# Where the tiles that TensorE reads begin in a partition: one residue modulo 512 bytes in place of several, in a two-layer decoder trunk

## The chip, the cores and the metric

The kernel runs on one core of a Trainium2 chip. The metric is the device time of one execution in microseconds (us). Before the change it is 2214.95 us, the median of three runs (2213.07 to 2218.6).

The core's engines run side by side, each on its own queue of instructions: TensorE (PE for its matmuls, PEld for its weight loads), VectorE (DVE), ScalarE (ACT), GpSimd (POOL) and SyncE (SP), which here issues most of the DMAs. The on-chip memory has 128 partitions; a tile takes the same range of bytes in each of them. TensorE multiplies a stationary operand (the weights, 128 columns) with a moving one (up to 512 columns here) and adds into a bank of the accumulation memory.

## The reference

A trunk of two layers on a sequence of 1024 positions of width 1024, all in float32. The first layer mixes by a gated linear recurrence, the second by sliding-window attention; each is followed by a layer norm, a gated FFN with a short causal convolution, and a second layer norm.

```python
for layer in range(DEPTH):
    if layer < N_A_LAYERS:
        mix = hgrn2_mixer(h, hgrn_w_in[layer], lower_bounds[layer],
                          hgrn_gnorm_w[layer], hgrn_w_out[layer])
    else:
        j = layer - N_A_LAYERS
        mix = swa_sink_mixer(h, k_shared, v_shared, swa_w_q[j], swa_sinks[j],
                             bias, mask, swa_w_out[j])
    h = layer_norm(ALPHA * h + mix, ln_mix_g[layer], ln_mix_b[layer])
    ff = conv_ffn(h, ffn_w_in[layer], ffn_conv_w[layer], ffn_conv_b[layer], ffn_w_out[layer])
    h = layer_norm(ALPHA * h + ff, ln_ffn_g[layer], ln_ffn_b[layer])
    if layer == N_A_LAYERS - 1:
        k_flat, v_flat = jnp.split(h @ shared_w_kv, 2, axis=-1)
        ...
```

`conv_ffn` multiplies 1024 × 1024 by 1024 × 5632, runs a causal convolution of width 3 over each channel, gates one half with the SiLU of the other, and multiplies 1024 × 2816 by 2816 × 1024. The mixers project with 1024 × 1024 matrices (four of them in the recurrence, two in attention, and one shared for keys and values).

## The kernel before

**Split products.** Every large operand is kept as two parts, a rounded one (`hi`) and the rest (`lo`), written by ScalarE (a copy, L203 or L158) and VectorE (a subtraction, L151). `mm3` (L175 to L178) makes one product of three matmuls: hi by hi (L176), hi by lo (L177), lo by hi (L178). These three lines issue 9288 of the matmuls, 7560 of them with 512 moving columns and 1728 with 256. TensorE's order is that of the program, written out by hand.

**Tiles and their places.** Pools lay tiles one behind the other in a partition, in the order of allocation; a tile's size is rounded up to 32 bytes. The pool `cp` (L100 to L110) comes first and stays: after a pad it holds

- T, 65,536 bytes, the activations transposed, hi and lo; it begins at byte 2048 of a partition
- Y, 32,768 bytes, at byte 67,584
- HL, at byte 100,352: the buffer of split weights, 12 × 1024 + 256 floats. It has six places of 8192 bytes, HL0 to HL5, each with a hi and a lo row of 1024 floats. `STARTS` (L134) puts place i at 2048 i floats plus 0, 16, 32, 64, 128 or 256 floats, so that in bytes modulo 512 they begin at 0, 64, 128, 256, 0 and 0
- small tiles (`ident`, parameters, masks), and a last pad of 8 floats

The pool `sm` follows with 1024 bytes of small tiles. All later pools begin behind it, at byte 154,304, which is 192 modulo 512: the recurrence's tiles (`hp`); for each FFN the extra weight tile HT (three rows of 4096 bytes), the raw loads `rx0` to `rx2` and TX (49,152 bytes, combinations of activations) or R in its place; and for attention the raw loads and the pool `at`, whose K and QB stand at 192, X and Vt at 256, and W, `q` and `bf` at 320 modulo 512.

**Stages**, in order of time: the recurrence over eight heads (projections `qf` and `ig_block`, and short matmuls of `recur` between them); its output projection (`out_proj`, L321); the FFN's up-projection (`Up`), its down-projection (`Down`); then keys, values and attention; output projection; `Up`; `Down`.

- In projections of the recurrence and of attention, T is moving (512 columns) and a place of HL holds the weights (`proj_T`, `q_proj`), or T holds the weights and HL is moving with 256 columns (`proj_tok`). Places are taken in turn (`ring`).
- In `out_proj`, the first half of the columns has T as weights and HL0 to HL3 moving; the second half has T as weights and TX moving.
- In `Up`, 22 blocks of columns (fc) each make seven products of twelve matmuls (a 2 × 2 scheme with seven products in place of eight). The order of products is 1, 2, 6, 7, 4, 5, 3. `weight_load` gives an even fc the pieces 8 to 14 (HL4 for products 1 and 2, HT for 6 and 7, HL5 for 4 and 5, HT again for 3), and an odd fc the pieces 0 to 6 (HL0, HL2, HL1, HL3). Moving is T, then TX for 6 and 7, T, and TX for 3.
- In `Down`, seven products over eleven chunks and four blocks of rows, three matmuls each, have both operands in one place of 1024 + 1024 floats: one of fifteen, six in HL, one in HT and eight in T.

**The tile `nsk`** (L1146, L1147) holds the negated sinks for attention. It is made on GpSimd from `sk`, which a DMA on ScalarE's queue brings (L1114, L1115), behind the loads of the layer norm's rows and of the shared weights, and behind the splits of these weights. `attend` reads it at L1233. On GpSimd's queue the memsets of QB (L1111) stand ahead of it, and the powers of the layer norm (`rs`, L225) behind it.

## Time and profile before

| | us |
|---|---|
| median of three runs | 2214.95 |
| lowest and highest | 2213.07, 2218.6 |
| the profiled execution | 2223.18 |
| its span, first to last instruction | 2221.4 |
| TensorE matmul busy in the span | 2175.4 |
| VectorE busy | 1786.9 |
| ScalarE busy | 941.6 |

Of the profiled execution 1.8 us lie outside its span. A row of the profile's groups names line, engine, operation, output and inputs by the program's tile names, with moving operand ahead of weights for a matmul; then shapes and count, busy time and mean duration, and idle time before with what ended it. Matmuls overlap in the pipeline, so their durations add up to more than the time that they take; the distance from one start to the next is what one costs, and it is read from the order of time. HL stands there for all of its places: which one is read follows from the order in the program. L12 is line 12 of the kernel.

### The profile page before, as it was taken

How to read it: one execution, taken by the hardware profiler on the slowest of the kernel's cores; microseconds unless marked ns; L12 is line 12 of the kernel's file. 1: busy time of each engine (PE TensorE's matmuls, PEld its weight loads, DVE VectorE, ACT ScalarE, POOL GpSimd, SP SyncE). 2: the span in 40 equal slices, each digit the busy share in tenths (PEclk: the TensorE clock that was granted, in tenths of full speed). 3: DMA queues.
4: the chain of work that ended last, by engine and by line, in shares of the span. 5: the costliest groups of instructions: out<-in, count | busy, mean ns of one | idle time of the engine just before them, and what ended most of it. 6: DMA issues, size and time to landing. Idle time of an engine off the chain costs nothing.

```text
span 2221.4 us, 33413 instructions
## 1 busy us (share of the span) xinstructions
PE 2175.4 (98%) x13135; PEld 1815.6 (82%) x13135; DVE 1786.9 (80%) x2415; ACT 941.6 (42%) x1625; POOL 178.5 (8%) x200
## 2 busy tenths in 40 slices
PE   8999999999999999999999999999999999999998
PEld 7888888978888888887888888777788888888887
DVE  2777665565789888888998778887799888889987
ACT  3333323332744443343333456764654443343431
POOL 0121111110100000000000012211000000000001
PEclk9999999999999999999999999999999999999999
DMA  6555443252222222238854421114222222249663
GB/s 196 187 194 172 153 171 115 62 126 91 86 85 85 84 79 86 85 102 264 276 168 133 114 89 34 34 56 135 76 95 94 74 79 86 86 143 314 207 213 132
DMA packets 231945, 281.16 MB, mean 127 GB/s; under 512 B 29978, under 2 KB 160747, under 8 KB 228971
## 3 DMA queue, kind: packets, MB, share of 16 engines
q1 hardware_dynamic: 228736, 276.53, 38.2%
q10 hardware_dynamic: 3050, 2.49, 0.8%
q8 instruction: 103, 1.69, 0.3%
q14 instruction: 56, 0.45, 0.1%
HBM read 213.96 MB, written 65.01 MB: 126 GB/s over the span
## 4 chain that ended last, share of the span: by engine, by line
PE 73%; DVE 14%; ACT 5%; DMA 4%; issue 3%; POOL 1%; SPq 0%; ACTq 0%; DVEq 0%; POOLq 0%
PE psmm L176 15%; PE psmm L178 15%; PE psmm L177 15%; PE psax L176 8%; PE psax L178 8%; PE psax L177 8%; PE psax L182 3%; DVE T L151 2%; DVE HL L151 1%; DMA rx<-in_ffn_w_in_dram 1%; PE psax L186 1%; DVE Y L481 1%; ACT Y L251 1%; ACT T L203 1%; DVE QB L1198 1%
## 5 line engine op out<-in xcount | busy, mean ns | idle before, releaser
L176 PE MATMUL psmm<-T,HL 128*128 128x512 f32 x768 | 309.9, 404 | 0.0
L177 PE MATMUL psmm<-T,HL 128*128 128x512 f32 x768 | 301.6, 393 | 3.8 <-issue 2.0
L178 PE MATMUL psmm<-T,HL 128*128 128x512 f32 x768 | 301.9, 393 | 0.0
L481 DVE SCALAR_TENSOR_TENSOR Y<-Y,cwt 128x1023 f32<-128x1023 f32 (+1 forms) x176 | 225.1, 1279 | 40.0 <-ACT Y L479 39.8
L479 ACT ACTIVATE Y<-Y,cwt 128x1024 f32<-128x1024 f32 x88 | 108.8, 1237 | 262.1 <-DVE Y L468 258.2
L176 PE MATMUL psmm<-HL,T 128*128 128x256 f32 (+1 forms) x656 | 199.6, 304 | 2.3 <-ACT T L203 2.3
L178 PE MATMUL psmm<-HL,T 128*128 128x256 f32 (+1 forms) x656 | 195.0, 297 | 2.4 <-DVE T L151 2.4
L177 PE MATMUL psmm<-HL,T 128*128 128x256 f32 (+1 forms) x656 | 194.7, 297 | 1.2 <-DVE HL L151 1.2
L203 ACT CAST HL<-rx 128x1024 fp32r<-128x1024 f32 (+1 forms) x137 | 140.2, 1043 | 125.6 <-DMA rx<-in_ffn_w_in_dram 35.0
L151 DVE TENSOR_TENSOR HL<-rx,HL 128x1024 fp32r<-128x1024 f32 (+1 forms) x137 | 165.6, 1212 | 16.0 <-ACT HL L203 15.4
L178 PEld LDWEIGHTS psmm<-T,HL 128*128 128x128 f32 x768 | 144.8, 189 | 35.2 <-issue 2.2
L177 PEld LDWEIGHTS psmm<-T,HL 128*128 128x128 f32 x768 | 145.3, 189 | 31.6 <-DVE T L151 2.7
L176 PEld LDWEIGHTS psmm<-T,HL 128*128 128x128 f32 x768 | 144.9, 189 | 31.7 <-issue 1.5
L176 PE MATMUL psax<-T,HL 128*128 128x512 f32 x352 | 138.3, 393 | 0.0
L178 PE MATMUL psax<-T,HL 128*128 128x512 f32 x352 | 137.9, 392 | 0.0
L177 PE MATMUL psax<-T,HL 128*128 128x512 f32 x352 | 137.6, 391 | 0.0
L176 PEld LDWEIGHTS psmm<-HL,T 128*128 128x128 f32 x656 | 125.5, 191 | 9.3 <-ACT T L203 2.9
L178 PEld LDWEIGHTS psmm<-HL,T 128*128 128x128 f32 x656 | 125.2, 191 | 6.7 <-DVE T L151 3.4
L225 POOL TENSOR_TENSOR rs<-rs,nhalf 128x1 f32<-128x1 f32 x32 | 25.7, 805 | 1295.5 <-DVE rs L224 1295.2
L177 PEld LDWEIGHTS psmm<-HL,T 128*128 128x128 f32 x656 | 125.5, 191 | 5.1 <-DVE HL L151 1.7
L860 POOL TENSOR_TENSOR kp<-kp,tot 128x512 f32<-128x512 f32 x48 | 72.9, 1519 | 293.4 <-PE psax L182 150.7
L151 DVE TENSOR_TENSOR HL<-raw,HL 128x1024 fp32r<-128x1024 f32 x51 | 64.0, 1254 | 23.2 <-ACT HL L158 23.1
(296 smaller groups left out, 5302.5 us busy)
## 6 DMA issues: line engine op xcount, KB each, us to landing
rx<-in_ffn_w_in_dram SPq DMA_DIRECT2D x136, 256.0 KB, 3.3
rx<-gd SPq DMA_DIRECT2D x118, 256.0 KB, 3.8
Y<-in_ffn_w_out_dram SPq DMA_DIRECT2D x44, 512.0 KB, 6.1
bsd<-Y SPq DMA_DIRECT2D x22, 1024.0 KB, 4.9
gd<-Y SPq DMA_DIRECT2D x44, 512.0 KB, 2.6
rx<-in_ffn_w_out_dram SPq DMA_DIRECT2D x54, 256.0 KB, 4.0
R<-bsd SPq DMA_DIRECT2D x44, 256.0 KB, 4.3
Y<-in_ffn_w_in_dram SPq DMA_DIRECT2D x40, 256.0 KB, 3.0
```

Of the source, the lines that this page charges most:

```text
L151: make = lambda e: e.tensor_tensor(lo, src, hi.bitcast(F32), op=ALU.subtract)
L176: nc.tensor.matmul(ps, st(0), mv(0), start=start, stop=False)
L177: nc.tensor.matmul(ps, st(0), mv(1), start=False, stop=False)
L178: nc.tensor.matmul(ps, st(1), mv(0), start=False, stop=stop)
L182: nc.tensor.matmul(ps, lhsT, rhs, start=start, stop=stop, **kw)
L186: nc.tensor.transpose(ps, src, ident)
L203: nc.scalar.copy(hi, src)
L225: nc.gpsimd.tensor_tensor(rs, rs, nhalf, op=ALU.pow)
L251: nc.scalar.activation(hf[:, kc, :], ps[:, k * P:(k + 1) * P], AF.Identity, bias=shift, scale=scale)
L479: nc.scalar.activation(c, u, AF.Identity, bias=cwt[:, l, 3, ci:ci + 1], scale=cwt[:, l, 2, ci:ci + 1])
L481: nc.vector.scalar_tensor_tensor(c[:, sh:], u[:, :S - sh], cwt[:, l, 2 - sh, ci:ci + 1], c[:, sh:], op0=ALU.mult, op1=ALU.add)
L860: (nc.gpsimd if i else nc.vector).tensor_tensor(kv[:, :, 0, :], kv[:, :, 0, :], tv[:, :, 1:2].to_broadcast([P, nb, m]), op=ALU.mult)
```

## The change

HL loses the 256 floats that spread its places, and the places are contiguous: 8192 bytes each from HL's start. The last pad of `cp` grows from 8 to 88 floats, so that together everything behind moves down by 704 bytes: the later pools begin at byte 153,600, a multiple of 512. In pool `at`, `nsk` is allocated (and made) right behind `sk`, and a pad of 96 floats follows, so that the 64 + 64 + 384 bytes make 512 and all that is allocated behind them stays on multiples of 512. T, Y and HL begin where they did. No other instruction changes.

```diff
-    HL = cp.tile([P, 12 * 1024 + 256], F32R, name="HL")
+    HL = cp.tile([P, 12 * 1024], F32R, name="HL")
...
-    cp.tile([P, 8], F32, name="pad1")
+    cp.tile([P, 88], F32, name="pad1")
...
-    STARTS = [2048 * i + o for i, o in enumerate((0, 16, 32, 64, 128, 256))]
-
     def hl_at(i):
-        return HL[:, STARTS[i]:STARTS[i] + 2048].rearrange("p (h n) -> p h n", h=2)
+        return HL[:, 2048 * i:2048 * (i + 1)].rearrange("p (h n) -> p h n", h=2)
...
         sk = at.tile([P, 16], F32, name="sk")
         nc.scalar.dma_start(sk, bass.AP(tensor=a["swa_sinks"].tensor, offset=0, ap=[[0, P], [1, 16]]))
+        nsk = at.tile([P, 16], F32, name="nsk")
+        nc.gpsimd.tensor_scalar(nsk, sk, -1.0, None, op0=ALU.mult)
+        at.tile([P, 96], F32, name="pad")
         place["hf"] = lambda tb: at.tile([P, KC, P], F32, name="q", bufs=3)
...
-        nsk = at.tile([P, 16], F32, name="nsk")
-        nc.gpsimd.tensor_scalar(nsk, sk, -1.0, None, op0=ALU.mult)
```

## The prediction

> **What bounds the kernel now.** I read the page's busy times first, then the windows by stage, then the order of time on TensorE, product by product.

> ```profile
> span 2221.4 us, 33413 instructions
> PE 2175.4 (98%) x13135; PEld 1815.6 (82%) x13135; DVE 1786.9 (80%) x2415; ACT 941.6 (42%) x1625; POOL 178.5 (8%) x200
> ...
> L176 PE MATMUL psmm<-T,HL 128*128 128x512 f32 x768 | 309.9, 404 | 0.0
> ```

> TensorE is busy for 98% of the span. A matmul of 512 columns is shown with 404 ns, but these overlap; what counts is the spacing, from one start to the next. In the windows below the columns are the stretch, then busy time (and count) of PE, PEld, DVE, ACT and POOL, the granted clock, the DMA share and GB/s.

> ```profile
> 0.00:565.00 565.00, 547.36 (x5393) 479.93 (x5394) 351.91 (x541) 192.18 (x412) 95.93 (x84) 0.99 0.45 146
> 617.70:1020.10 402.40, 402.24 (x1753) 328.55 (x1752) 359.14 (x402) 169.73 (x192) 0.00 (x0) 1.00 0.29 92
> 1238.00:1536.00 298.00, 287.60 (x1846) 240.94 (x1845) 239.24 (x467) 167.37 (x481) 54.25 (x78) 1.00 0.24 70
> 1614.35:2000.40 386.05, 385.75 (x1682) 315.01 (x1680) 346.00 (x386) 164.58 (x188) 0.00 (x0) 1.00 0.30 95
> ```

> Rows two and four are the up-projections of the two FFNs, 788.45 us together: TensorE is never without work and at full clock, and VectorE needs 359.14 of 402.40 us. Only the spacing of matmuls can shorten these stages. In the first row (recurrence) and the third (attention) TensorE stands idle for 17.6 and 10.4 us.

> One pair of column blocks, an even and an odd fc, shows how the spacing goes with the place that is read. These are the first matmuls of each stretch, start and duration ahead; only the sixth row is not a first one but the eleventh of the stretch that begins at 885.14.

> ```profile
> 866.02 0.39 PE L176 MATMUL psmm<-T,HL 128*128 128x512 f32 x1
> 871.48 0.39 PE L176 MATMUL psax<-TX,HT 128*128 128x512 f32 x1
> 876.93 0.39 PE L176 MATMUL psmm<-T,HL 128*128 128x512 f32 x1
> 882.41 0.39 PE L176 MATMUL psax<-TX,HT 128*128 128x512 f32 x1
> 885.14 0.39 PE L176 MATMUL psax<-T,HL 128*128 128x512 f32 x1
> 887.45 0.39 PE L177 MATMUL psax<-T,HL 128*128 128x512 f32 x1
> 890.63 0.40 PE L176 MATMUL psmm<-TX,HL 128*128 128x512 f32 x1
> 896.14 0.39 PE L176 MATMUL psax<-T,HL 128*128 128x512 f32 x1
> 901.74 0.39 PE L176 MATMUL psmm<-TX,HL 128*128 128x512 f32 x1
> 904.54 0.39 PE L176 MATMUL psax<-T,HL 128*128 128x512 f32 x1
> ```

> Call the start of a tile in its partition modulo 512 bytes its residue. T is at 0; TX and HT are at 192; the places of HL are at 0, 64, 128, 256, 0, 0. By `weight_load` the even block reads HL4, HT, HL5, HT and the odd one HL0, HL2, HL1, HL3. The stretches are 24, 24, 24, 12, then 24, 24, 24, 12 matmuls, so the spacings are:
> - moving and weights at the same residue: T with HL4 5.46/24 = 227.5 ns, TX with HT 227.1, T with HL5 228.3, TX with HT 227.5, T with HL0 5.49/24 = 228.8;
> - at different residues: TX with HL2 (192, 128) 5.51/24 = 229.6, T with HL1 (0, 64) 5.60/24 = 233.3, TX with HL3 (192, 256) 2.80/12 = 233.3.

> Inside the T–HL0 stretch, ten spacings take 2.31 us (231 ns) and the remaining fourteen, up to 890.63, take 3.18 (227.1). A stretch that follows a change of residue thus runs unsettled for some ten matmuls and then settles. Where the place changes and the residue does not, nothing is lost:

> ```profile
> 609.55 0.39 PE L176 MATMUL psmm<-T,HL 128*128 128x512 f32 x1
> 612.27 0.39 PE L176 MATMUL psmm<-T,HL 128*128 128x512 f32 x1
> 614.99 0.39 PE L176 MATMUL psmm<-T,HL 128*128 128x512 f32 x1
> 617.71 0.39 PE L176 MATMUL psmm<-TX,HT 128*128 128x512 f32 x1
> ```

> Here HL0, HL4 and HL0 again are read with T, twelve matmuls each, in 2.72 us each: 226.7 ns. That is my price for a settled 512-column matmul, and it is the smallest that any stretch here holds.

> **The change part by part.** After it T, HL (all six places), HT, TX, the recurrence's tiles, K, q, Vt, X and W all begin at residue 0. No matmul, copy or DMA is added or removed; only places move, and one GpSimd instruction.

> *Up-projections.* A pair of blocks is 168 matmuls. It takes 904.54 − 866.02 = 38.52 us; at 226.7 ns it takes 38.09, so 0.43 us go. The 788.45 us hold 20.5 such pairs: **−8.8 us**, all on the path, since TensorE has no idle time there. The cover of VectorE's 359.14 us of work shrinks by about 4.4 us in the first of them and suffices.

> *Output projections, second half* (weights in T, moving in TX: 0 and 192), 128 calls of `mm3`, 384 matmuls:

> ```profile
> 1556.70 0.39 PE L177 MATMUL psmm<-TX,T 128*128 128x512 f32 x1
> 1561.82 0.40 PE L178 MATMUL psmm<-TX,T 128*128 128x512 f32 x1
> ```

> 22 spacings in 5.12 us are 232.7 ns. Each run of 24 follows transposes, so some of its matmuls may stay unsettled: between 384 × (232.7 − 231) = 0.7 and 384 × 6.0 = 2.3 us. I take **−1.8**. The 384 matmuls with T as weights and HL as moving (first half) read HL0 to HL3, three of them off residue: between 0 and 288 × 6.6 = 1.9; I take **−0.8**, as HL2 and HL3 need not cost what HL1 does.

> *Down-projections*, 154 runs of twelve. Both operands lie in one place, so residues agree, but places follow each other with changes of residue:

> ```profile
> 1022.84 0.39 PE L176 MATMUL psmm<-HL 128*128 128x512 f32 x1
> 1025.56 0.39 PE L176 MATMUL psmm<-HT 128*128 128x512 f32 x1
> 1028.29 0.39 PE L176 MATMUL psmm<-HL 128*128 128x512 f32 x1
> 1031.05 0.39 PE L176 MATMUL psmm<-HL 128*128 128x512 f32 x1
> ```

> HL5 after HL4 takes 2.72 us, HT then 2.73, HL0 after HT 2.76. Some five of the fifteen places follow a change: 51 runs × 0.04 us = 2.1 us at most, 0 at least; I take **−1.8**, near the row.

> *Recurrence and attention, T moving*: 768 + 480 matmuls on places taken in turn, half of them off residue.

> ```profile
> 314.82 0.40 PE L177 MATMUL psmm<-T,HL 128*128 128x512 f32 x1
> 317.15 0.40 PE L178 MATMUL psmm<-T,HL 128*128 128x512 f32 x1
> ```

> HL1 here has 2.33/10 = 233 ns. Short matmuls stand between the runs of twelve, and after each the spacing may start unsettled, so 624 × 6.3 = 3.9 us is the most and 0 the least; I take **−1.7**.

> *Matmuls of 256 columns* go the other way. The first two rows are HL1 (64), the others HL5 (0):

> ```profile
> 243.36 0.28 PE L176 MATMUL psmm<-HL,T 128*128 128x256 f32 x1
> 244.66 0.28 PE L178 MATMUL psmm<-HL,T 128*128 128x256 f32 x1
> 287.47 0.28 PE L176 MATMUL psmm<-HL,T 128*128 128x256 f32 x1
> 288.79 0.28 PE L178 MATMUL psmm<-HL,T 128*128 128x256 f32 x1
> ```

> Eleven spacings take 1.30 and 1.32 us: 118.2 against 120.0 ns. Of 1728 such matmuls half read an off-residue place: between 0 and 864 × 1.8 = 1.6 us; I take **+0.8**.

> *The smaller matmuls* (K, q, X, W, Vt and the recurrence's) are no longer than 256 columns; at the 1.8 ns of the last rows the 256 of K with q would move 0.5 us to either side. I take 0.

> *Other engines.* VectorE's subtraction takes the same over all places of HL together and for HT:

> ```profile
> L151 DVE TENSOR_TENSOR HL<-rx,HL 128x1024 fp32r<-128x1024 f32 x135 | 164.3, 1219 | 16.0 <-ACT HL L203 15.4 <-DMA rx<-in_ffn_w_out_dram 0.2
> ...
> L151 DVE TENSOR_TENSOR HT<-rx,HT 128x1024 fp32r<-128x1024 f32 x29 | 35.4, 1220 | 2.4 <-ACT HT L203 2.4
> ```

> DMA into `rx` (192 now, 0 later) lands in 3.3 us, into Y (0) in 3.0; a load that is 0.3 us earlier moves nothing while TensorE always has its next product:

> ```profile
> rx<-in_ffn_w_in_dram SPq DMA_DIRECT2D x136, 256.0 KB, 3.3
> ...
> Y<-in_ffn_w_in_dram SPq DMA_DIRECT2D x40, 256.0 KB, 3.0
> ```

> *The moved `nsk`.* It goes ahead of the row loads and weight loads on SP's queue and of the weight splits on ScalarE and VectorE; none of these is on GpSimd's own queue, where it stays between the memsets of QB and the next `rs`:

> ```profile
> 1229.26 2.25 POOL L1111 MEMSET QB<- 64x512 f32 x4 [17.13 <-DVE T L151]
> 1235.60 0.27 POOL L1147 TENSOR_SCALAR nsk<-sk 128x16 f32<-128x16 f32 x1 [4.10 <-DMA sk<-in_swa_sinks_dram]
> 1236.15 0.57 POOL L225 TENSOR_TENSOR rs<-rs,nhalf 128x1 f32<-128x1 f32 x1 [0.27 <-DVE rs L224]
> ```

> It waits for the same landing of `sk` as now, and what is queued behind it, `rs`, became ready 0.27 us after it had ended. 0 us; without that cover the layer norm would be late by up to the 0.27 us of `nsk` itself.

> *Sum.* −8.8 − 1.8 − 0.8 − 1.8 − 1.7 + 0.8 = −14.1 us. In the recurrence and attention some of their 1.7 us turns into longer waits for other engines (the idle 17.6 and 10.4 us): +0.6 back. **−13.5 us**. The profiled execution took 2223.18 us, so 2209.7 for it; it lies 0.4% above the median of 2214.95, to which I apply the same difference: **2201 us**. With each term at its ends the gain is 6.8 to 19.5 us, so 2195 to 2208.

> **The rivals.**
> - *The unsettled starts stay* (they would come from the change of tile, not of residue). Then only steady mismatches go: per pair of blocks 24 × (233.3 − 228.3) + 24 × (229.6 − 227.1) + 12 × (233.3 − 227.5) = 0.25 us, 5.1 us in all; with 1.8 + 0.4 + 0 + 1.2 − 0.8 of the other terms 7.7 us: 2207. For it: a start costs something even where the operands agree. Against it: HL0–HL4–HL0 above and HL5 after HL4.
> - *The change does not do what it says for TensorE*: the spacing belongs to something else of HL1, HL3 and T–TX, as which buffer was written just before. Then 2215. Against it: TX with T is slow and TX with HT is not, T with HL1 is slow and T with HL0 is not. [...]
> - *Slower: a wrong settled state.* HL1 holds 233 ns over whole runs. If agreeing residues can settle into that state as well, nothing shakes it out once no residue changes, and a whole stage keeps it. At 233.3 in all of the up-projections a pair takes 39.19 us, +0.67 × 20.5 = +13.7, less the 4.7 us of the other terms: 2224. It makes the kernel slower than now from the point where the share of up-projection matmuls held there passes 0.6 (mean 230.7 between 226.7 and 233.3). Against it: each stretch with agreeing residues quoted here averages at most 230 ns.

> **How the numbers follow.** Forecast 0.66, unsettled starts stay 0.16, no effect 0.10, wrong state 0.06, anything else 0.02. The forecast's own range is 2195 to 2208; with a spread of the medians and most of the first rival, 8 in 10 lie between 2194 and 2210. A measurement of this kernel tells 0.3% (6.6 us) from no change: faster is below 2208.3. That holds 0.65 of the forecast, 0.11 of the first rival and 0.01 of the rest: 0.77; within 0.3%: 0.01 + 0.05 + 0.09 = 0.15; slower: 0.01 + 0.06 + 0.01 = 0.08.

> **What would show it.** Right: a pair of blocks in the up-projections takes 38.1 us, T with HL1 spaces at 227 like T with HL0, TX with T falls from 232.7 below 230, no ten unsettled matmuls after a change between T and TX, and 256-column matmuls are all at 120. Wrong: a pair at 38.25 (first rival), 38.5 (second), 39 or more (third); or the pair is right and the end is not, with longer waits on TensorE in recurrence or attention.

## The result, and the profile after

| | before | after |
|---|---|---|
| median, us (six runs each) | 2215.44 | 2204.24 |
| lowest and highest | 2213.07, 2219.57 | 2200.35, 2205.82 |
| profiled execution | 2223.18 | 2201.14 |
| its span | 2221.4 | 2199.3 |

The ratio is 0.9943, with a 95% interval of 0.9929 to 0.9957: 12.6 us less (9.5 to 15.7); the two medians are 11.2 us apart. The code is two lines shorter ahead of `mm3`, so that L174 to L176 are now what L176 to L178 were. The page's busy times, after:

```profile
PE 2154.9 (98%) x13135; PEld 1813.7 (82%) x13135; DVE 1782.7 (81%) x2415; ACT 942.3 (43%) x1625; POOL 179.3 (8%) x200
```

The share of TensorE is the same 98% of a shorter span, with the same number of matmuls. The windows over the two up-projections, after:

```profile
612.30:1010.30 398.00, 397.73 (x1753) 328.77 (x1752) 357.53 (x401) 169.92 (x192) 0.00 (x0) 1.00 0.29 92
1598.25:1979.85 381.60, 381.51 (x1682) 315.31 (x1682) 344.47 (x386) 164.91 (x188) 0.00 (x0) 1.00 0.30 96
```

They went from 402.40 to 398.00 and from 386.05 to 381.60 us, 8.85 us together, with the same 1753 and 1682 matmuls. The order of time on TensorE shows where it came from. First matmuls of stretches in one pair of blocks, after:

```profile
857.99 0.39 PE L174 MATMUL psmm<-T,HL 128*128 128x512 f32 x1
887.91 0.39 PE L174 MATMUL psax<-T,HL 128*128 128x512 f32 x1
893.35 0.39 PE L174 MATMUL psmm<-TX,HL 128*128 128x512 f32 x1
896.07 0.39 PE L174 MATMUL psax<-T,HL 128*128 128x512 f32 x1
```

The pair takes 896.07 − 857.99 = 38.08 us. T with HL1 (from 887.91) takes 5.44 us for 24 matmuls and TX with HL3 (from 893.35) 2.72 for twelve, both 226.7 ns; each was at 233.3. No stretch starts unsettled: the 132 matmuls of the pair ahead of them take 29.92 us, 226.7 ns too. Two more places, the second half of an output projection (TX with T) and a down-projection (HT, then HL0, then HL1):

```profile
1540.80 0.39 PE L175 MATMUL psmm<-TX,T 128*128 128x512 f32 x1
1545.82 0.39 PE L176 MATMUL psmm<-TX,T 128*128 128x512 f32 x1
...
1015.75 0.39 PE L174 MATMUL psmm<-HT 128*128 128x512 f32 x1
1018.47 0.39 PE L174 MATMUL psmm<-HL 128*128 128x512 f32 x1
1021.19 0.39 PE L174 MATMUL psmm<-HL 128*128 128x512 f32 x1
```

The 22 spacings of TX with T fell from 232.7 to 5.02/22 = 228.2 ns; what is left above 226.7 stands in the first of them behind the transposes: eight spacings up to 1542.65 take 1.85 us (231 ns), the remaining fourteen 3.17 (226.4). HT and HL0 take 2.72 us each, the settled time.

Over the whole trace, the mean distance from the start of a matmul of `mm3` to the next start, spacings over 262 ns (512 columns) or 150 ns (256) left out as waits, steps behind short matmuls and half-clock stretches. The count is the mean of the two traces:

| moving, weights | count | before, ns | after, ns | together, us |
|---|---|---|---|---|
| up-projections | 3424 | 229.30 | 226.71 | −8.9 |
| down-projections | 1822 | 228.14 | 226.82 | −2.4 |
| TX, T | 371 | 233.30 | 227.60 | −2.1 |
| HL, T, 512 columns | 361 | 230.98 | 227.98 | −1.1 |
| T, HL in recurrence and attention | 1320 | 229.94 | 228.37 | −2.1 |
| TX, HL and TX, HT ahead of the up-projections' windows | 72 | 228.68 | 226.67 | −0.1 |
| 256 columns | 1638 | 119.25 | 119.77 | +0.9 |

The sum is −15.8 us. The two profiled spans differ by more, 22.1 us, mainly because the clock differed too. The mean granted clock of the two executions, before and then after, and one stretch of the first:

```profile
core 0: 2221.4 us, clock 0.997
```

```profile
core 0: 2199.3 us, clock 0.999
```

```profile
306.40:309.90 3.50, 3.50 (x10) 2.70 (x9) 0.62 (x1) 0.00 (x0) 0.00 (x0) 0.51 0.63 255
```

A granted clock of 0.51 over 3.50 us is about 3.4 us at half clock. The starts at 306.52 and 306.95 are 0.43 us apart, where settled ones are 0.227; I estimate from this that the stretch cost half of its length, 1.7 us. The profiled execution of before holds three such stretches (from 306.5, 446.4 and 1043.7 us, with 0.51, 0.52 and 0.52 over 3.50 us each), that of after none until its last matmuls (1.00 from 20 to 2190 us): 5.1 of the 22.1 us. The clock does not belong to the change: the kernel after, profiled again (e10 below), has a mean of 0.997 too, with 10.2 us in such stretches by my count.

### The profile page after: what moved, and what is told of

It reads as the page before. It is cut to its first block, busy times and chain, and to the rows that moved or that the text cites. A ratio compares the mean times of both kernels' runs of the same rounds, so it can differ in the third digit from the quotient of the medians.

```text
span 2199.3 us, 33413 instructions
## 1 busy us (share of the span) xinstructions
PE 2154.9 (98%) x13135; PEld 1813.7 (82%) x13135; DVE 1782.7 (81%) x2415; ACT 942.3 (43%) x1625; POOL 179.3 (8%) x200
## 4 chain that ended last, share of the span: by engine, by line
PE 68%; DVE 18%; ACT 5%; DMA 4%; issue 3%; POOL 1%; SPq 0%; ACTq 0%; DVEq 0%; POOLq 0%
PE psmm L174 14%; PE psmm L176 14%; PE psmm L175 14%; PE psax L174 7%; PE psax L176 7%; PE psax L175 7%; PE psax L180 3%; DVE T L149 3%; DVE HL L149 2%; DVE Y L647 1%; PE psax L184 1%; ACT T L201 1%; DMA rx<-in_ffn_w_in_dram 1%; ACT Y L249 1%; DVE Y L599 1%
## 5 line engine op out<-in xcount | busy, mean ns | idle before, releaser
L174 PE MATMUL psmm<-T,HL 128*128 128x512 f32 x768 | 306.9, 400 | 0.0
L176 PE MATMUL psmm<-T,HL 128*128 128x512 f32 x768 | 299.5, 390 | 0.0
L174 PE MATMUL psmm<-HL,T 128*128 128x256 f32 (+1 forms) x656 | 199.7, 304 | 2.4 <-ACT T L201 2.4
L176 PE MATMUL psmm<-HL,T 128*128 128x256 f32 (+1 forms) x656 | 195.2, 298 | 2.4 <-DVE T L149 2.4
L176 PEld LDWEIGHTS psmm<-T,HL 128*128 128x128 f32 x768 | 144.2, 188 | 32.5 <-issue 1.7
L174 PEld LDWEIGHTS psmm<-T,HL 128*128 128x128 f32 x768 | 144.3, 188 | 30.3 <-issue 1.2
L174 PE MATMUL psax<-T,HL 128*128 128x512 f32 x352 | 137.3, 390 | 0.0
L176 PE MATMUL psax<-T,HL 128*128 128x512 f32 x352 | 137.0, 389 | 0.0
L174 PEld LDWEIGHTS psmm<-HL,T 128*128 128x128 f32 x656 | 126.1, 192 | 9.2 <-ACT T L201 3.0
L176 PEld LDWEIGHTS psmm<-HL,T 128*128 128x128 f32 x656 | 126.0, 192 | 6.6 <-DVE T L149 3.4
L201 ACT CAST HT<-rx 128x1024 fp32r<-128x1024 f32 (+1 forms) x51 | 44.0, 862 | 89.0 <-PE psmm L175 29.9
## 6 DMA issues: line engine op xcount, KB each, us to landing
rx<-in_ffn_w_in_dram SPq DMA_DIRECT2D x136, 256.0 KB, 3.2
rx<-gd SPq DMA_DIRECT2D x118, 256.0 KB, 3.6
rx<-in_ffn_w_out_dram SPq DMA_DIRECT2D x54, 256.0 KB, 4.1
R<-bsd SPq DMA_DIRECT2D x44, 256.0 KB, 4.4
Y<-in_ffn_w_in_dram SPq DMA_DIRECT2D x40, 256.0 KB, 3.0
```

The source lines that it names most:

```text
L174: nc.tensor.matmul(ps, st(0), mv(0), start=start, stop=False)
L176: nc.tensor.matmul(ps, st(1), mv(0), start=False, stop=stop)
L201: nc.scalar.copy(hi, src)
```

## The experiments

Each edit is against the kernel after, unless it says otherwise. The place of HL that an edit names is in bytes modulo 256.

### Is it the multiple of 512, or where the tiles stand to each other?

Everything is moved by 64 bytes:

```diff
-    cp.tile([P, 224], F32, name="pad0")
+    cp.tile([P, 240], F32, name="pad0")
```

> Every tile of the kernel after is moved up by 64 bytes (pad0 grows by 16 floats), so nothing begins at a multiple of 512 any more but all operands of a matmul still agree modulo 512. Theory (the relation of the two operands sets the spacing): as the kernel after, 2204 us, ratio to before 0.994, a pair of column blocks 38.1 us. Rival (it is the multiple of 512 itself that counts): spacings of 230 to 233 ns as with HL1 before, a pair of 39 us, 2220 us or more.

Measured: 2206.89 us, ratio 0.9958 (0.9945 to 0.997), which is the kernel after within the intervals. Its pair of blocks:

```profile
861.13 0.39 PE L174 MATMUL psmm<-T,HL 128*128 128x512 f32 x1
899.21 0.39 PE L174 MATMUL psax<-T,HL 128*128 128x512 f32 x1
```

38.08 us again, with none of these tiles at a multiple of 512 bytes. The common shift of 64 bytes changed nothing here (38.08 us in both), so what matters in this kernel is how the tiles stand to each other.

The change is then split in two: the places of HL alone (the later pools stay at 192), and the later pools alone (HL stays spread):

```diff
-    cp.tile([P, 88], F32, name="pad1")
+    cp.tile([P, 264], F32, name="pad1")
```

> HL's six places are contiguous at residue 0, but the later pools stay at residue 192 (pad1 264 floats). Theory (relation): TX with HL2, HL3 (192 against 0) at 233 ns, T with HL1 at 228.4, TX with T still 233, so a pair of blocks about 38.5 us and a gain of only 2 to 4 us: 2212 us. Rival (each misplaced tile costs by itself): HL1 to HL3 were the worst, so the larger part of the gain, 7 us or more: 2208 us, a pair of 38.25 us.

```diff
-    HL = cp.tile([P, 12 * 1024], F32R, name="HL")
+    HL = cp.tile([P, 12 * 1024 + 256], F32R, name="HL")
...
+    STARTS = [2048 * i + o for i, o in enumerate((0, 16, 32, 64, 128, 256))]
...
-        return HL[:, 2048 * i:2048 * (i + 1)].rearrange("p (h n) -> p h n", h=2)
+        return HL[:, STARTS[i]:STARTS[i] + 2048].rearrange("p (h n) -> p h n", h=2)
```

> HL stays spread as before, the later pools begin at residue 0 (with nsk and its pad as in the kernel after). Theory (relation): T with HL1 stays at 233.3 ns, TX with HL2 (0, 128) at 232, TX with T falls to 227.5, a pair of blocks 38.4 us, gain 4 to 5 us: 2211 us; together with e2 6 to 8 us, well short of the 11 to 13 of the whole change. Rival (each tile by itself): e2 and e3 add up to the whole, so 5 us here if e2 has 7.

Measured: 2213.21 us, 0.9989 (0.998 to 0.9998), and 2212.58 us, 0.9988 (0.9979 to 0.9997). The two parts bring 0.11% and 0.12%, the whole 0.57%. In the first one, TX with HL2, T with HL1, TX with HL3:

```profile
884.35 0.39 PE L174 MATMUL psmm<-TX,HL 128*128 128x512 f32 x1
889.95 0.39 PE L174 MATMUL psax<-T,HL 128*128 128x512 f32 x1
895.41 0.39 PE L174 MATMUL psmm<-TX,HL 128*128 128x512 f32 x1
898.21 0.39 PE L174 MATMUL psax<-T,HL 128*128 128x512 f32 x1
```

T with HL1 falls to 5.46/24 = 227.5 ns, but TX (192) with HL2 (0) rises to 5.60/24 = 233.3, where it was 229.6 with HL2 at 128. In the second one T (0) with HL1 (64) and TX (now 0) with HL3 (256):

```profile
890.90 0.39 PE L176 MATMUL psax<-T,HL 128*128 128x512 f32 x1
896.50 0.39 PE L176 MATMUL psmm<-TX,HL 128*128 128x512 f32 x1
899.23 0.39 PE L176 MATMUL psax<-T,HL 128*128 128x512 f32 x1
```

HL1 keeps its 5.60/24 = 233.3 ns; HL3 falls from 233.3 to 2.73/12 = 227.5. TX (0) with HL2 (128), the 24 matmuls from 885.31 up to the first of these rows, takes 5.59/24 = 232.9 ns. Tiles were put right, and yet some products got no better and TX with HL2 got worse in both halves (from 229.6 to 233.3 and 232.9): in these runs a spacing belongs to a pair of operands. So the gains of the halves do not add up to the whole, and the second part brought less than the 4 to 5 us that were expected of it.

### What is the period, and what does each distance cost?

All of HL at 256 bytes beside T and TX:

```diff
+    cp.tile([P, 64], F32, name="padh")
     HL = cp.tile([P, 12 * 1024], F32R, name="HL")
...
-    cp.tile([P, 88], F32, name="pad1")
+    cp.tile([P, 152], F32, name="pad1")
```

> As the kernel after, with HL moved up by 256 bytes: T, TX, HT at residue 0, all places of HL at 256. Theory A (the relation counts modulo 512): a spacing between 229 and 233 for T with HL and TX with HL, 2215 to 2225 us. Theory B (it counts modulo 256, as the settled 227 of T with HL3 before hints): settled at 226.7, at most unsettled starts when HL and HT follow each other, a pair of 38.1 to 38.4 us, 2204 to 2209 us.

Measured: 2203.25 us, 0.9941 (0.9927 to 0.9954); T with HL1 and TX with HL3:

```profile
887.94 0.39 PE L175 MATMUL psax<-T,HL 128*128 128x512 f32 x1
893.38 0.39 PE L175 MATMUL psmm<-TX,HL 128*128 128x512 f32 x1
896.10 0.39 PE L175 MATMUL psax<-T,HL 128*128 128x512 f32 x1
```

HL at 64, so that weights and moving operand are always apart in the up-projections but for HT:

```diff
+    cp.tile([P, 16], F32, name="padh")
...
-    cp.tile([P, 88], F32, name="pad1")
+    cp.tile([P, 200], F32, name="pad1")
```

> As the kernel after, with all six places of HL 64 bytes up: T, TX, HT at residue 0, HL at 64. Theory (relation modulo 256): T with HL and TX with HL at 233.3 ns everywhere, TX with HT and T with T unchanged, a pair of blocks 39.0 us, +18 us in the up-projections, +4 in recurrence and attention, -3 from the 256-column matmuls (118 ns): 2224 us, slower than the kernel before. Rival (places of equal residue are enough, as nothing changes from place to place): 2204 us, a pair of 38.1.

Measured: 2224.43 us, 1.0031 (1.0021 to 1.004), slower than before. One pair of blocks and the windows of both up-projections:

```profile
863.70 0.40 PE L175 MATMUL psmm<-T,HL 128*128 128x512 f32 x1
902.72 0.40 PE L175 MATMUL psax<-T,HL 128*128 128x512 f32 x1
```

```profile
612.85:1019.80 406.95, 406.95 (x1754) 329.24 (x1753) 359.57 (x402) 171.07 (x192) 0.00 (x0) 1.00 0.28 91
1608.50:1999.05 390.55, 390.53 (x1682) 315.61 (x1681) 346.26 (x386) 165.93 (x188) 0.00 (x0) 1.00 0.30 94
```

A pair takes 39.02 us; the two stages take 797.50 us, 17.9 more than in the kernel after (779.60). Only places differ between the two kernels: HL and the small tiles behind it stand 64 bytes further up, the later pools 512. e5's ratio to before is 1.0031, that of the kernel after 0.9943.

One execution with the six places at 16, 32, 96, 160, 224 and 240 bytes (HL grows by 128 floats for it) gives a map:

```diff
+    STARTS = [2048 * i + o for i, o in enumerate((4, 8, 24, 40, 56, 60))]
...
-        return HL[:, 2048 * i:2048 * (i + 1)].rearrange("p (h n) -> p h n", h=2)
+        return HL[:, STARTS[i]:STARTS[i] + 2048].rearrange("p (h n) -> p h n", h=2)
```

> As the kernel after, with HL's places at 16, 32, 96, 160, 224 and 240 bytes modulo 256, T, TX and HT at 0: one look that gives a spacing for each distance. Theory: only distance 0 settles at 226.7; 32 and 224 at 230 or more, 16 and 240 between 227 and 230, 96 and 160 at 231 to 233; time 2210 to 2225 us. Rival (only distances of whole 64 bytes collide): 16 and 240 at 226.7 or less.

Measured: 2222.56 us. T and TX stand at 0; the first rows are HL4 (224) and the HT behind it, then HL5 (240), HL0 (16), HL2 (96), HL1 (32), HL3 (160):

```profile
865.47 0.40 PE L176 MATMUL psmm<-T,HL 128*128 128x512 f32 x1
871.07 0.39 PE L176 MATMUL psax<-TX,HT 128*128 128x512 f32 x1
876.51 0.39 PE L176 MATMUL psmm<-T,HL 128*128 128x512 f32 x1
881.95 0.39 PE L176 MATMUL psax<-TX,HT 128*128 128x512 f32 x1
884.67 0.39 PE L176 MATMUL psax<-T,HL 128*128 128x512 f32 x1
890.11 0.39 PE L176 MATMUL psmm<-TX,HL 128*128 128x512 f32 x1
895.72 0.39 PE L176 MATMUL psax<-T,HL 128*128 128x512 f32 x1
901.32 0.40 PE L176 MATMUL psmm<-TX,HL 128*128 128x512 f32 x1
904.11 0.40 PE L176 MATMUL psax<-T,HL 128*128 128x512 f32 x1
```

24 matmuls (twelve in the last stretch) take 5.60 us at 224, 5.44 at 240, 5.44 at 16, 5.61 at 96, 5.60 at 32 and 2.79 at 160: 226.7 ns within 16 bytes of distance 0, and 232 to 234 at the other four. That 16 and 240 would be settled was the rival, not the theory; its reason, that only whole steps of 64 bytes collide, fails at 32, 96, 160 and 224. HL at 192 is the one distance between:

```diff
+    cp.tile([P, 48], F32, name="padh")
...
-    cp.tile([P, 88], F32, name="pad1")
+    cp.tile([P, 168], F32, name="pad1")
```

> As e5 with HL at 192. Theory: weights 64 bytes behind the moving operand modulo 256, as TX with HL2 before: 229.5 ns, a pair of blocks 38.5 us, +8 us there and +2 to 4 elsewhere: 2214 to 2216 us. Rival (the two directions cost the same): 233.3 ns, 2224 us as in e5.

Measured: 2208.79 us, 0.9955 (0.994 to 0.9971), better than expected. T with HL1 here:

```profile
886.37 0.39 PE L175 MATMUL psax<-T,HL 128*128 128x512 f32 x1
891.87 0.39 PE L175 MATMUL psmm<-TX,HL 128*128 128x512 f32 x1
```

5.50/24 = 229.2 ns. This was as expected, and it refutes the rival, by which the two directions cost the same. The sign shows with the roles exchanged as well: in the first half of the output projections HL moves and T holds the weights, and these matmuls space at 229.2 ns with HL at 64 (e5, weights 192 ahead) and at 233.3 with HL at 192 (e7, weights 64 ahead), as means over the trace. What made the kernel faster than expected are mainly the 256-column matmuls (HL moving, T as weights): their mean over the trace fell from 119.77 to 114.25 ns, 1638 × 5.5 = 9.0 us.

### The moved `nsk`

```diff
-        nsk = at.tile([P, 16], F32, name="nsk")
-        nc.gpsimd.tensor_scalar(nsk, sk, -1.0, None, op0=ALU.mult)
-        at.tile([P, 96], F32, name="pad")
+        at.tile([P, 112], F32, name="pad")
...
+        nsk = at.tile([P, 16], F32, name="nsk")
+        nc.gpsimd.tensor_scalar(nsk, sk, -1.0, None, op0=ALU.mult)
+        at.tile([P, 112], F32, name="pad2")
```

> The kernel after with nsk made where it was before (a second pad keeps the later tiles at residue 0). Theory: nsk's place in the program costs and gains nothing: 2204 us, ratio to before 0.994, nsk still runs right after sk's landing. Rival: 1 to 2 us of the difference are from nsk or the pool's new overlaps: 2206 us with longer waits of the layer norm at the start of attention.

Measured: 2203.11 us, 0.9934 (0.992 to 0.9947). The move shows no cost. GpSimd's order of time in the kernel after:

```profile
1221.19 0.28 POOL L1115 TENSOR_SCALAR nsk<-sk 128x16 f32<-128x16 f32 x1 [3.70 <-DMA sk<-in_swa_sinks_dram]
1222.07 0.57 POOL L223 TENSOR_TENSOR rs<-rs,nhalf 128x1 f32<-128x1 f32 x1 [0.61 <-DVE rs L222]
```

It waits for the landing of `sk` as before, and the `rs` behind it becomes ready 0.61 us after it has ended.

### A version that takes both gains

The e7 run suggests giving the 256-column matmuls a distance of their own. The places that are read as moving operands of 256 columns (`ig_block` and the values) begin at 192, all others at 0. HL grows to 6 × 2112 floats, and the pad behind `nsk` shrinks to 32 floats, which leaves the tiles behind it at 0 modulo 256:

```diff
-    def hl_at(i):
-        return HL[:, 2048 * i:2048 * (i + 1)].rearrange("p (h n) -> p h n", h=2)
+    def hl_at(i, o=0):
+        return HL[:, 2112 * i + o:2112 * i + o + 2048].rearrange("p (h n) -> p h n", h=2)
...
-            return split_raw(raw, eng).rearrange("p h (k c) -> p h k c", k=4)
+            return split_raw(raw, eng, 48).rearrange("p h (k c) -> p h k c", k=4)
...
```

> The kernel after, with two residues by use: places of HL that are moving operands of 256-column matmuls are written and read 192 bytes up, all else at distance 0 (places are 8448 bytes apart). Theory: those 1728 matmuls fall from 120 to 114 ns as in e7, the 512-column ones stay at 226.7 to 227.5, a pair of blocks 38.1 us; 10 us less on TensorE, of which the recurrence gives back some in waits: 2195 to 2199 us, about 6 us below the kernel after. Rival (TensorE only waits longer for the recurrence's other engines): 2202 to 2204 us with the same spacing.

Beside it on the same chip the kernel after once more:

> The kernel after once more, on the same chip as e9: 2203 to 2205 us, ratio to before 0.994.

Measured: 2200.10 us, 0.9931 (0.9918 to 0.9945), and 2204.99 us, 0.995 (0.9937 to 0.9962). Their intervals overlap, and the 2195 to 2199 us that were expected were not reached; the medians are 4.9 us apart. The 256-column matmuls in e9, two stretches of twelve:

```profile
226.42 0.28 PE L174 MATMUL psmm<-HL,T 128*128 128x256 f32 x1
227.83 0.28 PE L174 MATMUL psmm<-HL,T 128*128 128x256 f32 x1
...
236.30 0.28 PE L174 MATMUL psmm<-HL,T 128*128 128x256 f32 x1
237.66 0.28 PE L174 MATMUL psmm<-HL,T 128*128 128x256 f32 x1
```

1.41/12 = 117.5 ns in the first and 1.36/12 = 113.3 in the second: the same tiles at the same distance held two spacings. The mean is 115.71 against 119.77 in the kernel after, 1638 × 4.06 = 6.7 us, of which 4.9 reach the end by the medians; with overlapping intervals this gain is likely, not shown. The 512-column means are those of the kernel after.

An attempt at the same with all of HL at 16 (it grows by 128 floats):

```diff
-        return HL[:, 2048 * i:2048 * (i + 1)].rearrange("p (h n) -> p h n", h=2)
+        return HL[:, 2048 * i + 4:2048 * i + 2052].rearrange("p (h n) -> p h n", h=2)
```

> The kernel after with all places of HL 16 bytes up, T, TX and HT at 0. Theory (map of e6: 512-column matmuls still settle at 226.7 at 16 bytes, 256-column ones fall to 117.5): 4 us less in 1728 matmuls, 1 us back where HL moves against T: 2200 to 2203 us. Rival (with every place at 16 the settled state is lost, as at 32): T with HL near 233 ns, 2220 us.

Measured: 2207.37 us, 0.9964 (0.995 to 0.9977); the expectation failed. T with HL1 in an up-projection, then T with HL0 in the recurrence (fourth and twelfth matmul of a stretch), then HL0, HL1, HL2 in a down-projection:

```profile
889.35 0.39 PE L174 MATMUL psax<-T,HL 128*128 128x512 f32 x1
894.79 0.39 PE L174 MATMUL psmm<-TX,HL 128*128 128x512 f32 x1
...
307.73 0.39 PE L174 MATMUL psmm<-T,HL 128*128 128x512 f32 x1
309.60 0.39 PE L176 MATMUL psmm<-T,HL 128*128 128x512 f32 x1
...
1020.02 0.39 PE L174 MATMUL psmm<-HL 128*128 128x512 f32 x1
1022.78 0.39 PE L174 MATMUL psmm<-HL 128*128 128x512 f32 x1
1025.54 0.39 PE L174 MATMUL psmm<-HL 128*128 128x512 f32 x1
```

In the up-projection the spacing is 226.7 ns. In the recurrence T with a place at the same 16 bytes takes 1.87/8 = 233.8: one distance shows two spacings, and what decides between them is not shown. And HL0 with itself, at distance 0, takes 2.76/12 = 230.0, and so does HL1 behind it. In e5, with HL at 64, HL1 and HL2 together take 5.44 us, the settled 226.7 ns:

```profile
1030.73 0.39 PE L175 MATMUL psmm<-HL 128*128 128x512 f32 x1
...
1036.17 0.39 PE L175 MATMUL psmm<-HL 128*128 128x512 f32 x1
```

So the distance alone does not explain what starts at 16 bytes cost here (226.7 and 233.8 ns at 16, 230.0 at 0).

### Is the spacing the same in each execution?

> The kernel before, unchanged, profiled once more. Its first profiled execution took 2223.18 us, 7.7 above its median of 2215.44, and the spacing of matmuls in it lies 16.0 us above that of the kernel after, where the medians differ by 12.6. Theory A (the spacing is set by the places alone and is the same in every execution): up-projections again at a mean of 229.3 ns, 256-column matmuls at 119.2, and the sum of spacings again 16.0 us (within 0.5) above the kernel after; the execution takes 2213 to 2218, and what it is shorter by than 2223 lies in waits and half-clock windows, none of it in spacing. Theory B (unsettled stretches differ from one execution to the next): the sum of spacings is nearer to 12.6, 2 us or more below that of the first profile, with the up-projections at 229.0 ns or less.

Measured: 2219.45 us; up-projections 229.31 ns, 256 columns 119.21, down-projections 228.13, TX with T 233.32. None of these four means is off the first profile's by more than 0.04 ns. On the spacing theory A holds in these two executions and theory B falls; the time lies above the 2213 to 2218 us that theory A expected.

## Why the prediction was right

It gave 2201 us with a range of 2194 to 2210, and faster as the likeliest; measured were 2204.24 us, and 12.6 us less by the ratio where it had 13.5. By its steps:

- **Up-projections, −8.8 us**: 8.85 us by the windows, and a pair of blocks at 38.08 where 38.09 was predicted. The price of a settled matmul, 226.7 ns, was right, and VectorE's work stayed covered: TensorE is busy 397.73 of 398.00 us there.
- **TX with T, −1.8**: −2.1. **HL with T, −0.8**: −1.1. **Recurrence and attention, −1.7**: −2.1. Each lies inside the bounds that were given for it, a little beyond the value that was taken.
- **Down-projections, −1.8**: −2.4, beyond the end of 2.1 us that was given for it. It took all 154 places as runs of twelve. By `product` of `Down` only 80 are read so: the last chunks of a product (four or five, in one product all eleven) take turns, three matmuls each. In the kernel before, 34 of the 80 runs of twelve and 135 of the 296 runs of three follow a change of residue; from before to after the first kind lost 0.8 us in all and the second 1.5. A change within HL counts too: HL1, at 64 behind HL0 at 0, starts unsettled and takes 2.76 us, from 1031.05 (a row of the prediction) to the first matmul of HL2:

```profile
1033.81 0.39 PE L176 MATMUL psmm<-HL 128*128 128x512 f32 x1
```

- **256 columns, +0.8**: +0.9, now all near 120 ns. The sign was right, but a mean of 119.77 is above those of the other distances (114.25 in e7, 115.71 in e9).
- **Nothing for `nsk`, nothing for the smaller matmuls and other engines**: e8 bears out the first; the others were not measured by themselves.
- **Sum of the spacings, −14.1**: −15.8. It was mis-sized by 1.7 us in all, most of it in the down-projections and in recurrence and attention.
- **Waits, +0.6**: not resolved. The four profiled spans, less 1.7 us for each 3.4 us at half clock by my count (mean granted clocks of 0.997 and 0.997 before, 0.999 and 0.997 after), are 2221.4 − 5.1 and 2217.6 − 3.4 before, 2199.3 and 2204.9 − 5.1 after: means of 2215.2 and 2199.5, 15.7 us apart, with single pairs from 14.4 to 17.0, so that in the mean of the profiled executions the 15.8 us reached the end. The timed runs give 12.6 (9.5 to 15.7), and with e10's 0.995 some 11 us. The clock explains about 1 us by an estimate from its means: it averaged 0.9981 in 54 timed runs of before and 0.9976 in eleven of after. The rest of the gap stays open; two executions of before were profiled, and both took longer than its median. That 13.5 came so near to 12.6 is therefore in part luck: the spacings fell by more than forecast, and less of it shows in the timed runs than the 0.6 us for waits allows.

The rivals: *unsettled starts stay* (2207 us, pair 38.25) is refuted by the pair at 38.08 and by HT–HL0–HL1 without a start. In the down-projections of before, too, 45 runs of twelve that follow another place of the same residue average 226.7 ns, and the 34 that follow a change 229.2. *No effect on TensorE* (2215) is refuted by e5 and by the windows. *A wrong settled state* (2224) did not come in the kernel after, but something like it occurs: e11 shows T with HL at 16 at 226.7 and at 233.8 ns. The price of 39.19 us for a pair that runs at 233.3 was near: e5, where the products with HL do and those with HT do not, has 39.02. That its time, 2224.43 us, meets the rival's 2224 is chance, since its other terms differ.

Where the prediction's picture was wrong is the rule itself. It asked whether the residues of the two operands agree modulo 512 bytes, and brought every tile to a multiple of 512 for it. e1 shows that a common shift by 64 bytes did not matter (a pair at 38.08 us), e2 and e3 that the distance of the two operands did (T with HL1 at 227.5 and at 233.3 ns), e4 that 256 bytes cost what 0 does (226.7), and e5 and e7 that 64 bytes ahead cost more than 64 behind (233.3 and 229.2). For starts at 16 bytes the distance was not all (226.7 and 233.8 in e11). The change hit the right distance all the same, since with all tiles at 0 every distance is 0, and no place follows another with a change; the second is what the down-projections gain their 2.4 us by, where weights and moving operand lie in one place in both kernels. What shows the mechanism is the spacing at each distance; how the memory or the reads of TensorE produce it was not tried, and no run here can show it.

## What to carry to other kernels

Where TensorE never waits, read the distance from one matmul's start to the next by pair of tiles. If 512-column products of one kind hold 233 ns and others 227, as here, look at where the weights and the moving operand begin: in this kernel the same residue modulo 256 bytes gave 226.7 ns and weights 64 bytes ahead 233.3, while a residue of 16 for HL gave 226.7 or 233.8 (e11). Whether another kernel shows the same is to be measured there. Do it for whole pairs, since moving one tile right moved its other partner wrong (TX with HL2 from 229.6 to 233.3 and 232.9 ns in e2 and e3), and measure short moving operands apart from long ones, as for 256 columns another distance had the lower mean (115.71 ns in e9 against 119.77).

## What was not expected of the hardware

- In these runs the spacing of 512-column matmuls went with (start of weights − start of moving operand) modulo 256 bytes: 226.7 ns at 0 (after, e4; but 230.0 for HL with itself in e11, where its places begin at 16), 229.2 at 192 (e7), 232 to 234 at 64 (e5), 128 (e3), 32, 96, 160 and 224 (e6), and at 16 and 240 either 226.7 (e6) or more (up to 233.8 at 16 in e11). By places alone this kernel gained 0.57% (the change) or lost 0.31% (e5).
- For 256 columns the order was different: a mean of 119.77 ns at distance 0 (after), and 117.5 or 113.3 in two stretches with the moving operand at 192 and the weights at 0 (e9).
- The granted clock fell to half for 3.4 us three times in the profiled execution of before (0.51, 0.52 and 0.52 over 3.50 us), behind pauses of TensorE of 2.04, 1.98 and 2.02 us (the last with another of 0.76 behind it). In that of after it stayed at 1.00 up to 2190 us. The pause ahead of the stretch that was shown at 306.40:

```profile
306.04 0.40 PE L177 MATMUL psmm<-T,HL 128*128 128x512 f32 x1 [2.04 <-issue]
...
306.52 0.63 PE L176 MATMUL psmm<-T,HL 128*128 128x512 f32 x1
```

After 2.04 us without a matmul the third one already takes 0.63 us instead of 0.39. In the kernel after a pause of 1.86 us, up to 443.45 us, was followed by no such stretch (a clock of 1.00 from 440 to 452 us), while in e11 a pause of 1.73 us, up to 302.09 us, was followed by matmuls of 0.63 us from 303.37 us on. So in these executions the length of the pause alone does not decide; what does was not shown.
